# Dilated attention scores in one piece per unit, and a new projection order, in a two-layer hybrid encoder

## The chip, the cores and the metric

The kernel runs on one core of a Trainium2 chip. The metric is the device time of one launch in microseconds (us). Three runs of the kernel before the change took 927.87, 928.56 and 929.92 us; the median, 928.56 us, is the number that the change is measured against.

## The reference

Two encoder layers over 512 positions of width 1024, then a final RMSNorm. A layer normalizes x, projects it once into many parts, runs two attention branches over them, gates each branch and projects back:

```python
h = rms_norm(x, norm_g[layer])
p = h @ w_in[layer]
c_q, c_kv, k_r, gate_a, dil_qkv, gate_b = jnp.split(p, split_points, axis=-1)
a = mla_attention(c_q, c_kv, k_r, ...) * jax.nn.silu(gate_a)
b = dilated_attention(dil_qkv, cos_d, sin_d) * jax.nn.silu(gate_b)
x = x + jnp.concatenate([a, b], axis=-1) @ w_out[layer]
```

The latent branch has 8 heads; queries and keys come from low-rank latents (384 and 256 wide) that get an RMSNorm of their own. The dilated branch has 3 groups of 8 heads of 64, with windows and dilations (128, 1), (512, 4) and (2048, 16); the groups' outputs are weighted by their softmax denominators and added. Everything is float32, to float32 accuracy.

## The kernel before, in words

Activations lie transposed: chunks of 128 features by 512 positions. To keep accuracy, each operand is split into a high and a low part (ACT makes the high part at L221, DVE the low part at L222), and each product is three matmuls (`triple`, L241 to L243: high by high, high by low, low by high). So a projection of 128 output features from 1024 inputs is 24 matmuls of 512 columns in one PSUM bank. PSUM has 8 banks, and all of them come from one pool (`bank()`, bufs=8): who asks for a ninth waits until the oldest has been read.

Weights are fetched three tiles ahead of their use (`prefetch`, L188 to L205, AHEAD = 3): SP loads the raw tile (L195), ACT makes the high part (L198), and the low part comes either from DVE (L203) or, for the projections in `ADDED` after the place `FROM` in the plan, from ACT (L200) and an accumulating transfer on the POOL queue (L201).

Dilated heads go in units: 12 in a layer, each with two heads of one group. Units of the first group are "near" (`near_scores` L653, `near_out`), of the other two "far" (`far_scores` L727, `far_out` L769). For each unit the main line makes the queries and the keys (`dil_qk`); there is one buffer of keys (`kst`), so the next unit's keys wait until this unit's scores are done. The scores are matmuls with 64 rows (L673 near; L744 and L747 far), two heads beside each other in two banks. A unit's scores come in two parts: a near part is 12 matmuls, a far part 8, each with 2 banks. DVE and ACT then turn scores into exponentials (L680, L750, L753 and others). The outs transpose the exponentials (L449), split them again (`pt`, L221 and L222) and multiply them with the values (L550 near, L785 far); a far unit has four such products, and behind each of them ACT copies half of a bank (L788) and DVE adds twice (L789, L791). `combine` (L818) and `combine_last` (L837) weight and add the groups. `mla_out` does the same for a pair of latent heads ("mo").

At the end of a layer `out_part` (L849) projects the mixed outputs, 24 matmuls to a chunk of x, and `out_add` (L840) takes the result: it fetches the old chunk into one of two buffers (`xl`, bufs=2), adds (DVE, L845), stores (L846), makes the high part (ACT, L273) and the low part (DVE, L274) for the next layer, and squares it (ACT, L264; added up on POOL, L268). The next layer begins with `latent_first` (L364): its matmuls (L376) take the eight chunks one after the other as they come.

The order of all this on TensorE is not that of the layers' formulas. `Weave.run` (L84 to L136) takes the projections from a main line, in the order that `forward_order()` (L29, L30) lists, and puts the other work between them from side lines: norms (`nline`), scores (`sline`), outs (`tline`), and combinations with the latent outputs among them (`cline`). A task on a side line is released when what it needs was finished a given lag ago, counted in modelled microseconds (LD 8.25 for dilated scores, LM 2.0 for latent scores, LG 6.0 and LG2 16.5 for outs, LAG 2.5 for most others), and a credit (RATE, CAP) limits how much side work may stand between projections. Where the main line is blocked, side tasks go ahead of their lags (`force`). Inside a side line the order is fixed, so a task that is not ready holds up those behind it.

At the start eleven matmuls on zeros (L296, WARM) run while the first loads arrive. ACT's queue issues the load of the first raw weights, of the norm gains (`gn`), and of the second raw weights.

Of the kernel before, what the change touches and what calls it, by code (L numbers as in the profile page):

```python
# [7 lines left out]
F32 = mybir.dt.float32  # L8
# [3 lines left out]
ALU = mybir.AluOpType  # L12
# [11 lines left out]
STEP, LD0, WARM, LG2, LY = 2, 10.0, 11, 16.5, 5.0  # L24
LV = 3.0
# [3 lines left out]
def forward_order():  # L29
    return [('ckv',), ('v', 1, 0), ('cq', 2), ('cq', 0), ('cq', 1), ('dqk', 0, 0), ('dqk', 0, 1), ('nv', 0), ('mur', 0), ('ga', 0), ('dqk', 1, 0), ('kr',), ('dqk', 1, 1), ('nv', 1), ('muq', 0), ('muk', 0), ('mv', 0), ('muq', 1), ('dqk', 2, 1), ('muk', 1), ('dqk', 2, 0), ('muq', 2), ('dqk', 3, 1), ('muq', 3), ('dqk', 3, 0), ('dqk', 4, 1), ('mur', 1), ('v', 2, 0), ('muq', 4), ('dqk', 4, 0), ('dqk', 5, 0), ('muk', 2), ('ga', 1), ('muq', 5), ('dqk', 5, 1), ('mv', 1), ('dqk', 6, 0), ('nv', 2), ('gb', 0), ('muq', 6), ('dqk', 6, 1), ('muq', 7), ('nv', 3), ('dqk', 8, 0), ('gb', 1), ('muk', 3), ('v', 1, 1), ('ga', 2), ('dqk', 7, 0), ('dqk', 7, 1), ('dqk', 10, 0), ('dqk', 8, 1), ('dqk', 9, 0), ('dqk', 9, 1), ('v', 2, 1), ('dqk', 10, 1), ('ga', 3), ('dqk', 11, 0), ('dqk', 11, 1), ('gb', 2), ('gb', 3)]  # L30
# [27 lines left out]
FROM = PLAN.index(("dqk", 0, 1, 1))  # L58
# [79 lines left out]
def hybrid_encoder(ctx, tc, xT, wst, gains, fgain, tables, keytab, masks, out):  # L138
# [9 lines left out]
    def t(shape, dtype, tag, bufs):  # L148
        uid[0] += 1
        return sb.tile(shape, dtype, name=f"{tag}_{uid[0]}", tag=tag, bufs=bufs)  # L150
# [137 lines left out]
    load_w(nc.scalar, 0)  # L288
    nc.scalar.dma_start(gn, gains)
    load_w(nc.scalar, 1)  # L290
# [362 lines left out]
    def near_scores(L, u, part):  # L653
# [5 lines left out]
        if part == 0:  # L659
            L.st0[p] = t([128, 4, 4], F32, "st0", 2)  # L660
        st = L.st0[p]
        banks = [bank() for _ in range(2)]
        for j in range(2):
            i = 2 * part + j
# [9 lines left out]
        for j in range(2):  # L674
            i = 2 * part + j
# [11 lines left out]
        if part:  # L687
            by_residue(L, p)
        yield 0.9, 1.0
# [37 lines left out]
    def far_scores(L, u, part):  # L727
# [7 lines left out]
        pt = t([128, S], F32, "p", 8)  # L735
        p4 = pt.rearrange("p (j a x) -> p j a x", j=2, a=2)
        banks = [bank() for _ in range(2)]
        by4 = lambda x: x.rearrange("p j (x y) -> p j x y", y=4)
        for j in range(2):
            b = 2 * part + j  # L740
# [7 lines left out]
        for a in range(2):  # L748
# [394 lines left out]
```

## Time and profile before

| what | value |
|---|---|
| median of three runs | 928.56 us (927.87 to 929.92) |
| the profiled execution, its own time | 929.99 us |
| span of its instructions | 928.2 us |
| mean granted TensorE clock | 0.996 |

The page's first part gives each engine's busy time as a share of the span. A row of a list of instructions has the start in us, the time from start to end in us, the engine, the line, the operation, what it writes and reads, and how many equal ones follow each other (x12); a bracket at its end is a wait just before it and what ended it. A row of the waits has the sum of a releaser's waits in us, their number, and the mean. A row of the grouped instructions has the sum of busy us and the mean ns of one, then the idle us before them. In the list by tiles three numbers stand for the shortest, the median and the longest ns.

### The profile page before, as it was taken

To read this page: it belongs to the slowest core of one execution; us is meant where nothing else is said; L and a number is where in the kernel's file an instruction comes from. 1 tells how busy PE (TensorE), PEld (TensorE's weight loads), DVE (VectorE), ACT (ScalarE), POOL (GpSimd) and SP (SyncE) were. 2 spreads that over 40 slices of the span, in tenths; PEclk is the share of its full clock that TensorE was granted. 3 is DMA by queue.
4 is the path that set the end of the run, shared out by engine and by line. 5 is a ranking of instruction groups with operands and counts; after the bars stand their busy time and mean duration, and the time that the engine had idled before them with its cause. 6 is when DMAs were issued, how large, how long until landed. Compare 5 with 4: busy or idle time off the path is not lost.

```text
span 928.2 us, 15855 instructions
## 1 busy us (share of the span) xinstructions
PE 908.0 (98%) x5175; PEld 773.4 (83%) x5175; DVE 692.4 (75%) x1733; ACT 597.6 (64%) x1449; POOL 313.2 (34%) x365
## 2 busy tenths in 40 slices
PE   9999999999999999999999999999999999999996
PEld 7978888988889889887897888889888888898785
DVE  6756787877868776688766679787878676767964
ACT  6546876667757766764445468756768586676533
POOL 0134253345542432233211343524464234224300
PEclk9999999999999999999999999999999999999998
DMA  8457453276554764664453653615667558367542
GB/s 271 121 124 146 97 123 69 65 163 148 122 124 93 148 125 107 137 155 132 166 169 95 146 121 82 126 40 134 138 126 158 129 101 167 78 142 138 147 125 91
DMA packets 86466, 118.14 MB, mean 127 GB/s; under 512 B 16944, under 2 KB 37232, under 8 KB 86384
## 3 DMA queue, kind: packets, MB, share of 16 engines
q1 hardware_dynamic: 66656, 81.59, 30.6%
q0 software_dynamic: 19296, 35.14, 24.0%
q8 instruction: 41, 0.67, 0.3%
q10 hardware_dynamic: 432, 0.41, 0.1%
q14 instruction: 41, 0.34, 0.1%
HBM read 112.74 MB, written 4.36 MB: 126 GB/s over the span
## 4 chain that ended last, share of the span: by engine, by line
PE 83%; DVE 8%; ACT 4%; issue 2%; DMA 1%; POOL 1%; ACTq 0%; DVEq 0%; POOLq 0%
PE bank L241 22%; PE bank L242 22%; PE bank L243 22%; PE bank L449 5%; PE bank L550 3%; PE bank L376 3%; PE bank L744 1%; PE bank L785 1%; PE bank L673 1%; DVE pt L222 1%; DVE whl L203 1%; ACT whl L198 1%; DMA p<-wst 1%; DMA wraw<-wst 1%; DVE tmp L630 1%
## 5 line engine op out<-in xcount | busy, mean ns | idle before, releaser
L241 PE MATMUL bank<-hl,whl 128*128 128x512 f32 x712 | 283.9, 399 | 2.2 <-ACT hl L221 1.3
L242 PE MATMUL bank<-hl,whl 128*128 128x512 f32 x712 | 278.3, 391 | 0.0
L243 PE MATMUL bank<-hl,whl 128*128 128x512 f32 x712 | 278.1, 391 | 0.0
L198 ACT CAST whl<-wraw 128x512 fp32r<-128x512 f32 (+3 forms) x243 | 143.8, 596 | 121.2 <-PE bank L243 80.2
L201 POOL DMA_DIRECT2D whl<-wst x134 | 117.9, 884 | 225.2 <-ACT whl L200 152.7
L243 PEld LDWEIGHTS bank<-hl,whl 128*128 128x128 f32 x712 | 133.6, 188 | 29.5 <-DMA whl<-wst 0.4
L241 PEld LDWEIGHTS bank<-hl,whl 128*128 128x128 f32 x712 | 133.7, 188 | 28.5 <-ACT hl L221 1.7
L242 PEld LDWEIGHTS bank<-hl,whl 128*128 128x128 f32 x712 | 134.0, 188 | 23.9 <-DVE hl L222 0.3
L241 PE MATMUL bank<-whl,hl 128*128 128x256 f32 (+2 forms) x328 | 99.6, 304 | 1.6 <-ACT hl L221 1.6
L243 PE MATMUL bank<-whl,hl 128*128 128x256 f32 (+2 forms) x328 | 97.9, 298 | 0.0
L242 PE MATMUL bank<-whl,hl 128*128 128x256 f32 (+2 forms) x328 | 97.7, 298 | 0.0
L628 POOL TENSOR_TENSOR tmp<-tmp,sd 128x512 f32<-128x512 f32 x48 | 63.2, 1316 | 91.9 <-DVE tmp L626 65.4
L203 DVE TENSOR_TENSOR whl<-wraw,whl 128x512 fp32r<-128x512 f32 (+3 forms) x109 | 76.6, 710 | 23.1 <-ACT whl L198 22.1
L222 DVE TENSOR_TENSOR pt<-bank,pt 128x512 fp32r<-128x512 f32 x128 | 83.6, 684 | 5.4 <-ACT pt L221 4.0
L200 ACT ACTIVATE whl<-wraw 128x512 fp32r<-128x512 f32 x134 | 85.0, 634 | 0.1
L221 ACT CAST pt<-bank 128x512 fp32r<-128x512 f32 x128 | 69.9, 588 | 10.7 <-PE bank L449 10.3
L530 POOL TENSOR_SCALAR p<-p,lc 128x512 f32<-128x512 f32 x64 | 48.8, 769 | 70.0 <-DVE lc L529 64.2
L449 PE MATMUL bank<-ident,p 128*128 128x128 f32 x512 | 67.7, 275 | 0.0
L241 PEld LDWEIGHTS bank<-whl,hl 128*128 128x128 f32 x328 | 62.3, 190 | 3.9 <-ACT hl L221 1.8
L243 PEld LDWEIGHTS bank<-whl,hl 128*128 128x128 f32 x328 | 62.3, 190 | 2.0 <-DVE hl L222 0.4
L242 PEld LDWEIGHTS bank<-whl,hl 128*128 128x128 f32 x328 | 62.4, 190 | 1.7
L449 PEld LDWEIGHTS bank<-ident,p 128*128 128x128 f32 x512 | 59.2, 142 | 5.4
(181 smaller groups left out, 1620.1 us busy)
## 6 DMA issues: line engine op xcount, KB each, us to landing
wraw<-wst SPq DMA_DIRECT2D x218, 256.0 KB, 3.1
whl<-wst POOLq DMA_DIRECT2D x134, 256.0 KB, 4.4
tmp<-shd SPq DMA_DIRECT2D x32, 128.0 KB, 4.3
xl<-xT SPq DMA_DIRECT2D x10, 256.0 KB, 2.9
wraw<-wst SPq DMA_DIRECT2D x16, 144.0 KB, 2.3
wraw<-wst SPq DMA_DIRECT2D x12, 192.0 KB, 2.6
x1d<-xl SPq DMA_DIRECT2D x8, 256.0 KB, 3.2
xl<-x1d SPq DMA_DIRECT2D x8, 256.0 KB, 3.2
```

Source lines behind the costliest of these rows:

```text
L198: nc.scalar.copy(hi, src)
L200: nc.scalar.mul(lo, src, -1.0)
L201: nc.gpsimd.dma_start(lo, wst[emitted[0], :, :c], accum_op=ALU.add)
L203: nc.vector.tensor_tensor(lo, src, F(hi), op=ALU.subtract)
L221: nc.scalar.copy(dst_hi, src)
L222: nc.vector.tensor_tensor(dst_lo, src, F(dst_hi), op=ALU.subtract)
L241: nc.tensor.matmul(a, w[:, 0], h[:, 0], start=first, stop=False)
L242: nc.tensor.matmul(a, w[:, 0], h[:, 1], start=False, stop=False)
L243: nc.tensor.matmul(a, w[:, 1], h[:, 0], start=False, stop=last)
L449: nc.tensor.transpose(b[:, 128 * i:128 * i + 128], x, ident)
L530: nc.gpsimd.tensor_scalar(pt, pt, l1, 0.0, op0=ALU.mult, op1=ALU.add)
L628: nc.gpsimd.tensor_tensor(u, u, L.sd, op=ALU.mult)
```

## The change

It has four parts.

1. **Scores of a dilated unit as one piece.** `near_scores` and `far_scores` no longer take a part: all 24 or 16 matmuls are issued in a row into four banks, and after them the vector work of both halves. The modelled cost that they report is that of two parts (1.8 and 0.9).
2. **Scores don't wait for values.** The scores of a latent head no longer need its values ("mv"), those of a dilated unit no longer need "v" or "nv". The outs need the values instead, with a lag LO = 4.0. The norm of the query latents waits a lag LQ = 5.0 after its projections, not LAG = 2.5. The latent outputs ("mo") get a line of their own (`gline`).
3. **Another list in `forward_order()`**, of the same projections. `FROM` is now the later of the first two key projections, and in the second layer the place of `load_ahead` is the later of ("gb", 2) and ("muq", 7).
4. **Start.** The load of `gn` goes out on the POOL queue, so ACT's queue has only the two loads of weights; WARM is 10, not 11.

In the parts of the diff below, the new list of projections is shown only by its start.

```diff
-STEP, LD0, WARM, LG2, LY = 2, 10.0, 11, 16.5, 5.0
-LV = 3.0
+STEP, LD0, WARM, LG2, LY = 2, 10.0, 10, 16.5, 5.0
+LV, LQ, LO = 3.0, 5.0, 4.0
...
-    return [('ckv',), ('v', 1, 0), ('cq', 2), ('cq', 0), ('cq', 1), ('dqk', 0, 0), ('dqk', 0, 1), ('nv', 0), ...
+    return [('ckv',), ('v', 1, 0), ('cq', 2), ('dqk', 0, 1), ('cq', 0), ('cq', 1), ('dqk', 0, 0), ('dqk', 1, 0), ...
...
-FROM = PLAN.index(("dqk", 0, 1, 1))
+FROM = max(PLAN.index(("dqk", 0, i, 1)) for i in range(2))
...
-    load_w(nc.scalar, 0)
-    nc.scalar.dma_start(gn, gains)
-    load_w(nc.scalar, 1)
+    nc.gpsimd.dma_start(gn, gains)
+    for k in range(2):
+        load_w(nc.scalar, k)
...
-    def far_scores(L, u, part):
+    def far_scores(L, u):
...
-        pt = t([128, S], F32, "p", 8)
-        p4 = pt.rearrange("p (j a x) -> p j a x", j=2, a=2)
-        banks = [bank() for _ in range(2)]
+        pts = [t([128, S], F32, "p", 8) for _ in range(2)]
+        both = [[bank() for _ in range(2)] for _ in range(2)]
...
-        for j in range(2):
-            b = 2 * part + j
+        for b in range(4):
+            banks, j = both[b // 2], b % 2
...
-        yield 0.44, 0.5
+        yield 0.9, 1.0
...
-    main, nline, sline, tline, cline = ([] for _ in range(5))
+    main, nline, sline, tline, cline, gline = ([] for _ in range(6))
...
-        task(nline, k("lcq"), later(*[k("cq", c) for c in range(3)], k("norm")), latent_norm, "cq")
+        task(nline, k("lcq"), [(k("cq", c), LQ) for c in range(3)] + later(k("norm")), latent_norm, "cq")
...
-                task(sline, k("s0", what, n), [(x, LM if what == "m" else LD0 if n == 0 else LD) for x in needs], scores, n, 0)
-                task(sline, k("s", what, n), now(*before[0]), scores, n, 1)
-                task(tline, k("o", what, n), [(k("s", what, n), LG2 if what == "d" and unit(n)[0] == 2 else LG)], f, n)
+                needs = [(x, LM if what == "m" else LD0 if n == 0 else LD) for x in needs]
+                if what == "m":
+                    task(sline, k("s0", what, n), needs, scores, n, 0)
+                    task(sline, k("s", what, n), now(*before[0]), scores, n, 1)
+                else:
+                    task(sline, k("s", what, n), needs + now(*before[0]), scores, n)
+                g, p = unit(n) if what == "d" else (0, 0)
+                values = k("mv", n // 4) if what == "m" else k("v", g, p // 2) if g else k("nv", p)
+                task(tline, k("o", what, n), [(k("s", what, n), LG2 if g == 2 else LG), (values, LO)], f, n)
...
-                task(cline, k(what, n), needs, f, n)
+                task(gline if what == "mo" else cline, k(what, n), needs, f, n)
```

What this does to the order can be read off the two programs. The number of matmuls on TensorE is the same but for the one on zeros: 5174 for 5175. The pieces of scores become fewer: 46 runs of score matmuls before, 24 after, one for each of the 12 units of two layers. Of the 46, four near units were in one piece of 24 already and four in two pieces of 12; 14 far units were in two pieces of 8 and two in three.

The first place is the scores of the last far unit of layer 0 on TensorE. Before, the second part of the scores (`bank_4888`, `bank_4889`) stands behind an out of another unit (L785) and the rest of a projection (L241 to L243 into `bank_4823`):

```order
L744 MATMUL bank_4849<-kst,q_4678 128x256
L744 MATMUL bank_4850<-kst,q_4678 128x256
L747 MATMUL bank_4849<-kst,q_4678 128x128
L747 MATMUL bank_4850<-kst,q_4678 128x128
L785 MATMUL bank_4869<-pt_4727,v_3594 128x256 x2
L241 MATMUL bank_4823<-hl_172,whl_4759 128x512
L242 MATMUL bank_4823<-hl_172,whl_4759 128x512
L243 MATMUL bank_4823<-hl_172,whl_4759 128x512
L241 MATMUL bank_4823<-hl_178,whl_4759 128x512
L242 MATMUL bank_4823<-hl_178,whl_4759 128x512
L243 MATMUL bank_4823<-hl_178,whl_4759 128x512
L744 MATMUL bank_4888<-kst,q_4678 128x256
```

After, the second half (`bank_4863`, `bank_4864`) follows the first (`bank_4861`, `bank_4862`) at once:

```order
L740 MATMUL bank_4861<-kst,q_4643 128x256
L740 MATMUL bank_4862<-kst,q_4643 128x256
L743 MATMUL bank_4861<-kst,q_4643 128x128
L743 MATMUL bank_4862<-kst,q_4643 128x128
L740 MATMUL bank_4863<-kst,q_4643 128x256
L740 MATMUL bank_4864<-kst,q_4643 128x256
L743 MATMUL bank_4863<-kst,q_4643 128x128
L743 MATMUL bank_4864<-kst,q_4643 128x128
```

What moved is the projection work that stood between the two halves; it now stands around the whole piece.

The second place is TensorE at the end of layer 0, where the last two far units' outs are (L785 before, L783 after; `pt` are split exponentials, `v` the values). Before, the four products of the last unit have output projections (L241 to L243) between them:

```order
L785 MATMUL bank_5173<-pt_5122,v_4389 128x256 x2
L785 MATMUL bank_5180<-pt_5122,v_4389 128x256 x2
L785 MATMUL bank_5187<-pt_5130,v_4389 128x256 x2
L241 MATMUL bank_4962<-hl_5147,hl_5009 128x512
L242 MATMUL bank_4962<-hl_5147,hl_5009 128x512
L243 MATMUL bank_4962<-hl_5147,hl_5009 128x512
L241 MATMUL bank_4980<-hl_5147,hl_5045 128x512
L242 MATMUL bank_4980<-hl_5147,hl_5045 128x512
L243 MATMUL bank_4980<-hl_5147,hl_5045 128x512
L785 MATMUL bank_5194<-pt_5130,v_4389 128x256 x2
```

After, the outs of units 10 and 11 follow each other, with only the transposes of unit 11 (L449) between them:

```order
L783 MATMUL bank_5107<-pt_5040,v_3647 128x256 x2
L783 MATMUL bank_5114<-pt_5040,v_3647 128x256 x2
L783 MATMUL bank_5121<-pt_5048,v_3647 128x256 x2
L783 MATMUL bank_5128<-pt_5048,v_3647 128x256 x2
L449 MATMUL bank_5135<-ident,p_4859 128x128 x4
L449 MATMUL bank_5143<-ident,p_4860 128x128 x4
L783 MATMUL bank_5152<-pt_5140,v_3648 128x256 x2
L783 MATMUL bank_5159<-pt_5140,v_3648 128x256 x2
L783 MATMUL bank_5166<-pt_5148,v_3648 128x256 x2
L783 MATMUL bank_5173<-pt_5148,v_3648 128x256 x2
L241 MATMUL bank_5180<-hl_2194,whl_5075 128x512
L242 MATMUL bank_5180<-hl_2194,whl_5075 128x512
```

Projections that stood between these outs stand earlier in the layer now. Five sums of output projections (`bank_4841`, `bank_4928`, `bank_4964`, `bank_4989` and `bank_5017`) are open all through these rows, so three of the eight banks go round: a row's bank is free once that of the third row above it has been read, and `bank_5180` once DVE's second add has read `bank_5159`. Right behind, where layer 1 begins: before, 115 matmuls of 512 columns stand between the last output projection of x's first chunk and the first use of its last chunk by layer 1. After, 77 of 512 and 26 of 288 columns stand there.

More of the change, by code (lines that the diff above doesn't have):

```diff
@@ L651, in dil_qk, with near_scores @@
         yield 0.65 * STEP, 0.0
-    def near_scores(L, u, part):
+    def near_scores(L, u):
         g, p = unit(u)
         q = L.q["d", u]
-        if part == 0:
-            L.st0[p] = t([128, 4, 4], F32, "st0", 2)
-        st = L.st0[p]
-        banks = [bank() for _ in range(2)]
-        for j in range(2):
-            i = 2 * part + j
+        st = L.st0[p] = t([128, 4, 4], F32, "st0", 2)
+        both = [[bank() for _ in range(2)] for _ in range(2)]
+        for i in range(4):
+            banks, j = both[i // 2], i % 2
             for x, (lq, lk) in enumerate(((0, 0), (0, 1), (1, 0))):
@@ L673, in near_scores @@
                     nc.tensor.matmul(so, q[r, lq, 128 * i:128 * i + 128], k, start=x == 0, stop=x == 2)
-        for j in range(2):
-            i = 2 * part + j
+        for i in range(4):
+            banks, j = both[i // 2], i % 2
             m = msk[:, 0:256] if i else msk[:, 256:512]
@@ L686, in near_scores @@
             L.p["d", u, i] = pt
-        if part:
-            by_residue(L, p)
-        yield 0.9, 1.0
+        by_residue(L, p)
+        yield 1.8, 1.0
     def by_residue(L, p):
@@ L734, in far_scores @@
         m = msk[:, 512:640].rearrange("p (x y) -> p x y", y=4) if g == 1 else msk[:, 640:644].unsqueeze(1).to_broadcast([128, 32, 4])
-        pt = t([128, S], F32, "p", 8)
-        p4 = pt.rearrange("p (j a x) -> p j a x", j=2, a=2)
-        banks = [bank() for _ in range(2)]
+        pts = [t([128, S], F32, "p", 8) for _ in range(2)]
+        both = [[bank() for _ in range(2)] for _ in range(2)]
         by4 = lambda x: x.rearrange("p j (x y) -> p j x y", y=4)
-        for j in range(2):
-            b = 2 * part + j
+        for b in range(4):
+            banks, j = both[b // 2], b % 2
             c = slice(128 * b, 128 * b + 128)
@@ L747, in far_scores @@
                 nc.tensor.matmul(so, q[64 * a:64 * a + 64, 1, c], kst[64 * a:64 * a + 64, 0, c], start=False, stop=True)
[L748 to L760 removed]
+        for part in range(2):
+            p4 = pts[part].rearrange("p (j a x) -> p j a x", j=2, a=2)
+            for a in range(2):
+                s = both[part][a].rearrange("p (j l x) -> p j l x", j=2, l=2)
+                nc.vector.tensor_tensor(by4(p4[:, :, a]), by4(s[:, :, 0]), m.unsqueeze(1).to_broadcast([128, 2, 32, 4]), op=ALU.add)
+                for j in range(2):
+                    b = 2 * part + j
+                    nc.vector.tensor_tensor_reduce(p4[:, j, a], s[:, j, 1], p4[:, j, a], -0.125, 3e38, ALU.add, ALU.min,
+                                                   st[:, b, a:a + 1])
+                for j in range(2):
+                    b = 2 * part + j
+                    nc.scalar.activation(p4[:, j, a], p4[:, j, a], AF.Exp, scale=-1.0, bias=st[:, b, a:a + 1],
+                                         accum_out=st[:, b, 2 + a:3 + a])
+            L.p["d", u, part] = pts[part]
+        if g == 2:
             shares(L, p)
@@ L998, in hybrid_encoder @@
         if last:
[L999 removed]
+            at = [i for i, x in enumerate(main) if x[0] in (k("gb", 2), k("muq", 7))][-1]
             line = []
```

21 lines of the change are left out of this document (4 added, 17 removed).

## The prediction

> **What bounds the kernel now.** I read the page first: which engine is busy.
>
> ```profile
> span 928.2 us, 15855 instructions
> PE 908.0 (98%) x5175; PEld 773.4 (83%) x5175; DVE 692.4 (75%) x1733; ACT 597.6 (64%) x1449; POOL 313.2 (34%) x365
> ```
>
> TensorE (PE) is busy for 908.0 of 928.2 us, and no other engine for more than 75%. So a gain can only come from PE's own time, which is not all at full rate, and from the 20 us around it. What PE waits for is in the second view, its waits by releaser; the ten longest are:
>
> ```profile
> PE bank L241 <- ACT hl L221: 2.9, 2, 1.6
> PE bank L256 <- POOL tmp L354: 1.8, 2, 0.9
> PE bank L296 <- DVE q L293: 1.5, 1, 1.5
> PE bank L744 <- ACT q L221: 1.4, 2, 0.7
> PE bank L550 <- ACT pt L221: 1.2, 2, 0.6
> PE bank L747 <- DVE q L222: 1.1, 2, 0.5
> PE bank L550 <- DVE pt L222: 0.9, 2, 0.4
> PE bank L241 <- DVE st L680: 0.9, 1, 0.9
> PE bank L785 <- DVE og L791: 0.7, 2, 0.4
> PE bank L376 <- ACT hl L273: 0.6, 2, 0.3
> ```
>
> All are small and come twice, once for each layer: the order leaves too little work between a producer and PE's use. A new order can take away each one, or put another in its place. The third view is PE's instructions one by one around scores:
>
> ```profile
> 237.65 0.39 PE L242 MATMUL bank<-hl,whl 128*128 128x512 f32 x1
> 237.88 0.39 PE L243 MATMUL bank<-hl,whl 128*128 128x512 f32 x1
> 238.19 0.38 PE L744 MATMUL bank<-kst,q 64*128 64x256 f32 x2
> 238.42 0.22 PE L747 MATMUL bank<-kst,q 64*128 64x128 f32 x2
> ...
> 238.64 0.22 PE L747 MATMUL bank<-kst,q 64*128 64x128 f32 x2
> 238.79 0.50 PE L241 MATMUL bank<-hl,whl 128*128 128x512 f32 x1
> 239.13 0.40 PE L242 MATMUL bank<-hl,whl 128*128 128x512 f32 x1
> ```
>
> Matmuls of 512 columns follow each other every 0.23 us, though each lasts 0.39 (the end overlaps the next). So a wait costs its idle time and about 0.16 us more, since the overlap is lost. A far piece of 8 takes 239.13 - 237.88 = 1.25 us, in which two matmuls of 512 (0.46) are; 0.79 is left. Of this a block (four matmuls) takes 0.22 (238.42 to 238.64); the rest is what entering and leaving the 64-row form costs.
>
> **The change, part by part.** The sum is made against the profiled execution's 929.99 us, which is 1.43 above the median.
>
> *Scores in one piece.* A far piece of 16 is 0.79 + 2 x 0.22 = 1.23 instead of 2 x 0.79 = 1.58: 0.35 saved, for 16 far units 5.6 us; the two third pieces save about 0.3 each, 0.6. The near pieces:
>
> ```profile
> 291.80 0.98 PE L673 MATMUL bank<-kst,q 64*128 64x256 f32 x12
> 292.71 0.50 PE L785 MATMUL bank<-pt,v 128*128 128x256 f32 x2
> ...
> 81.01 1.69 PE L673 MATMUL bank<-kst,q 64*128 64x256 f32 x24
> 82.63 0.50 PE L241 MATMUL bank<-hl,whl 128*128 128x512 f32 x1
> ```
>
> Twelve take 0.91, so two pieces 1.82; twenty-four take 1.62, and each piece has some 0.2 around it that is then paid once: 0.4 for each of 4 units, 1.5. Together -7.7. If the edges were half as dear it would be -5, with dearer near edges -8.5.
>
> *Waits in mid-layer.* Scores that don't need values, the lag LQ and the new order part the producers from their uses: the waits at L256, L744, L747, L550 (both) and L241 behind L680 are 1.8 + 1.4 + 1.1 + 1.2 + 0.9 + 0.9 = 7.3 us in 11 places. In the new order each of these pairs has 3 us or more of PE work between, where the longest of these waits is 0.9. With 11 x 0.16 that is -9.1. If a third stays under another name, -6.
>
> *Half clock.* The windows view has one dip of the granted clock, behind two such waits in layer 0; its twin in layer 1 has none:
>
> ```profile
> 135.00:140.00 5.00, 5.00 (x25) 0.67 0.55 97
> 131.53 0.38 PE L744 MATMUL bank<-kst,q 64*128 64x256 f32 x2
> 132.45 0.33 PE L747 MATMUL bank<-kst,q 64*128 64x128 f32 x2 [0.54 <-DVE q L222]
> 133.77 1.23 PE L550 MATMUL bank<-pt,v 128*128 128x256 f32 x7 [0.45 <-DVE pt L222]
> 138.75 0.40 PE L241 MATMUL bank<-kml,q 96*128 96x512 f32 x1
> ...
> 586.76 0.38 PE L744 MATMUL bank<-kst,q 64*128 64x256 f32 x2
> 592.43 0.39 PE L241 MATMUL bank<-kml,q 96*128 96x512 f32 x1
> ```
>
> In the first row the fourth number is the granted clock, 0.67. The same work takes 7.22 us here and 5.67 in layer 1. With the waits gone, so is the dip: -1.5, or 0 if the clock drops somewhere else.
>
> *Start.* `gn` is second on ACT's queue, and the first high part waits for it:
>
> ```profile
> 5.55 0.72 ACT L273 ACTIVATE hl<-og,gn 128x512 fp32r<-128x512 f32 x1 [1.11 <-DMA gn<-gains]
> 6.32 2.35 PE L376 MATMUL bank<-hl,hl 128*128 128x512 f32 x9 [0.32 <-ACT hl L273]
> ```
>
> PE's first projection follows that ACT instruction at once. On POOL's queue `gn` has nothing ahead of it, and the second raw weights move up one place. But what comes next, the weights and chunks, arrives hardly earlier, and PE had only 0.32 idle here. I take -0.3, between 0 and -0.6. The warm-up matmul left out ran in time that waits anyway: 0. POOL and ACT have nothing else queued then.
>
> *Ends of the layers.* The waits at L241 behind L221 (2.9, 2) and at L785 (0.7, 2) lie there, since outs of the last units stand too close; with 4 x 0.16 that is -4.2, as these spots are ordered anew. In their place:
>
> ```profile
> L789 DVE TENSOR_TENSOR tmp<-bank,tmp 64x256 f32<-64x256 f32 x64 | 26.9, 420 | 10.6 <-ACT tmp L788 9.6
> L791 DVE TENSOR_TENSOR og<-bank,tmp 64x256 f32<-64x256 f32 x64 | 26.9, 420 | 1.7
> L222 DVE TENSOR_TENSOR pt<-bank,pt 128x512 fp32r<-128x512 f32 x128 | 83.6, 684 | 5.4 <-ACT pt L221 4.0
> L837 DVE TENSOR_TENSOR og<-og,og 128x512 f32<-128x512 f32 x8 | 5.5, 686 | 0.2
> ...
> 438.42 0.87 PE L785 MATMUL bank<-pt,v 128*128 128x256 f32 x6
> 439.49 0.87 DVE L789 TENSOR_TENSOR tmp<-bank,tmp 64x256 f32<-64x256 f32 x2
> ...
> L845 DVE TENSOR_TENSOR xl<-xl,bank x8: 680/689/691, 447.2 to 469.2; 128x512 f32<-128x512 f32 x8
> L273 ACT ACTIVATE hl<-xl,gn x8: 709/724/727, 448.0 to 469.9; 128x512 fp32r<-128x512 f32 x8
> ```
>
> At layer 0's end the outs of units 10 and 11 now stand back to back, with three banks to go round. The projection behind them gets its bank when DVE has made 12 adds (12 x 0.42), two low parts (2 x 0.684) and one combination (0.686): 7.1 us. From the first product to DVE's first add are 439.49 - 438.42 = 1.07, and some 0.5 goes in gaps for ACT's copies: 8.6. PE's own work there, 16 products and 8 transposes, is 24 x 0.12 = 2.9 (six products take 0.87, the last one's end included). Stall: +5.7. It would be 3 if ACT and DVE overlap better than I take it, 8 if DVE is late with earlier work.
>
> At layer 1's start, x's eight chunks go through two buffers: from the first add at 447.2 to the end of the last high part, 469.9 + 0.72 = 470.6, are 23.4 us. Before, PE had 115 matmuls of 512 in that time (26.5 us) and waited only for the 0.6 at L376 shown above. After, it has 77 of 512 and 26 of 288 columns, 17.7 + 3.4 = 21.1. Stall: 23.4 + 0.4 for the ends of the first and last step - 21.1 = +2.7; 0 if the loads through the two buffers run faster with less beside them, 5 if the adds come later by the stall ahead.
>
> Not shown by the trace of before: new small waits at layer 1's end (0 to 1.6, I take 0.8), three spots in mid-layer where a producer is under 2 us ahead (0 to 3, 1.0), and a clock dip. For that the nearest row is the dip above: it came behind gaps of only 0.54 and 0.45, and cost 1.5; once, and not at its twin. The stretch of 9 us at layer 0's end has several gaps of about 1 us, so I take half of it: +0.8, between 0 and 1.7. The Trainium skill ("TensorE: Matmul & The Clock Gate", Part 1, "The HAM clock gate") has the half rate come only after an idle window of about 3.4 us. By that rule the new gaps would cost no clock, and the sum would be 0.8 lower; the row speaks against it, as no gap near it is over 0.54 us.
>
> Sum: -7.7 - 9.1 - 1.5 - 0.3 - 4.2 + 5.7 + 2.7 + 0.8 + 1.0 + 0.8 = -11.8. So 918.2 for the profiled execution, 916.8 against the median.
>
> **The rivals.**
>
> *Banks (slower).* A joined piece takes four of eight banks at once and gives back none before DVE has gone through the first. The price is in the waits: L241 behind L680 of a near unit's scores, 0.9 idle and 0.16. If each of the 20 newly joined units (16 far, 4 near) did this, it would be 20 x 1.06 = +21 us: 938. It turns the sign from 11 such waits on (11 x 1.06 = 11.7). For it: in the output projections five banks are held anyway. Against: in the new order the first bank asked back after a piece has at least 14 matmuls (3.2 us) ahead of it, and before, the one with 2.4 us of work waited 0.9 and those at 3.1 didn't. The Trainium skill ("TensorEngine Tiling (Array Packing)", "Gotcha 1: PSUM Pressure") warns that tiling by rows takes more banks at once; the one wait of 0.9 agrees. Chance 0.10.
>
> *Bunching gives half back.* Where outs and scores are in larger lumps, DVE, ACT and PE take turns at the ends of both layers, not of one. If layer 1's end, which has the same outs and output rows, stalls as layer 0's does (+5.7 instead of 0.8) and the chunks take their 5 instead of 2.7, that is +7.2: 924. For it: DVE is at 75%, and a unit's 8 adds come in one lump. Against: in layer 1 no next layer waits, and the order there has projections between the last outs. Chance 0.16.
>
> *The ends are cheap.* If the stall at layer 0's end is 3, layer 1's start costs nothing, and no small wait or dip comes up, it is -2.7 - 2.7 - 2.6 = 8 us less: 909. Chance 0.12.
>
> *The change does not do what it says.* The order of the changed program has the 24 pieces whole, so I give this nothing.
>
> **How the numbers follow.** My forecast has 0.62; its own range is 912 to 922, from the joined pieces (1.7 either way), the waits (2), the end of layer 0 (2.5), the start of layer 1 (2.5) and the rest (1.5), which are independent: the root of the sum of squares is 4.7. For 8 times in 10 the range also takes in the cheap ends and the bunching, with their own spread of about 2.5: 907 to 927. Left out are the banks (0.10) and some 0.08 at the edges. About 0.2% is what a measurement of this kernel tells from no change, so faster is below 926.7: the forecast 0.62, the cheap ends 0.12 and three quarters of the bunching, 0.86. The same (926.7 to 930.4): the rest of the bunching and a little of the banks, 0.05. Slower: the banks, 0.09.
>
> **What would show it.** In the changed profile: a piece of 16 far scores takes about 1.2 us, one of 24 near 1.6; PE's busy time falls by about 9 us (pieces and clock); the waits at L256, at the scores and at L550 are gone. At the end of layer 0 PE stands for 5 to 6 us among the outs of units 10 and 11, released by L222 and by DVE's reads of banks, and at the start of layer 1 L376 waits 2 to 3 us for L273. No other line has a wait of a joined piece's bank. I am wrong if the pieces save less than 5 us, if waits for banks stand behind most of the joined units, or if the stalls at the ends pass 15 us together.

## The result: 2.9% slower, and the profile after

The changed kernel took 955.55 us (median of 4 runs, 953.94 to 959.56) against 928.74 us before on the same chip; the ratio is 1.0294 with a 95% interval from 1.0275 to 1.0313. The forecast was 916.8 us. The profiled execution, whose lines follow, took 959.56 us and is the slowest of the four, at a mean granted clock of 0.982; the others had 0.985 to 0.987. By estimate its loss by the clock is 3 to 5 us more than theirs.

The page of the changed kernel:

```profile
span 957.7 us, 15886 instructions
PE 915.2 (96%) x5174; PEld 777.1 (81%) x5174; DVE 699.9 (73%) x1733; ACT 594.9 (62%) x1449; POOL 313.9 (33%) x366
```

Before, 928.2 - 908.0 = 20.2 us of the span were without PE work; now it is 957.7 - 915.2 = 42.5, 22.3 more. And PE is busy for 7.2 us more, though it has the same matmuls but for one of the warm-up. So there are two losses: PE waits more, and it works more slowly. PE's waits (sum in us, number, and the longest in us; the reading help ahead of the prediction calls the last number the mean, but it is the longest):

```profile
PE bank L243 <- DMA whl<-wst: 13.3, 5, 5.1
PE bank L376 <- ACT hl L273: 2.8, 2, 1.5
PE bank L241 <- POOL q L512: 2.5, 3, 1.4
PE bank L241 <- ACT hl L221: 2.1, 2, 1.9
PE bank L449 <- ACT ku L819: 1.5, 1, 1.5
PE bank L783 <- DVE st L751: 1.5, 1, 1.5
PE bank L296 <- DVE q L293: 1.5, 1, 1.5
PE bank L783 <- DVE og L789: 1.5, 1, 1.5
PE bank L243 <- DVE q L222: 1.4, 2, 0.8
PE bank L817 <- DVE st L751: 1.1, 1, 1.1
```

Of the waits that the forecast meant to lose in mid-layer, L256, both at L550 and L241 behind the near units' scores are gone; at the far units' scores (L740, before L744 and L747) 1.7 of 2.5 us are left, in other places. In their place stands a group of which the kernel before had 0.4 us: the third matmul of a triple, L243, waits for the low part of a weight tile (13.3 us in 5 places), which the accumulating transfer on the POOL queue brings. All of PE's waits together are 34.4 us in 29 places, before 13.0 in 18.

The slower work is in the windows of 5 us (length of the window, busy time of PE, PEld, DVE, ACT and POOL with counts, then granted clock, DMA share, GB/s):

```profile
85.00:90.00 5.00, 3.60 (x12) 2.90 (x12) 1.71 (x3) 0.90 (x3) 3.22 (x4) 0.64 0.83 175
90.00:95.00 5.00, 5.00 (x20) 4.22 (x20) 3.05 (x10) 2.58 (x7) 1.89 (x3) 0.68 0.20 35
...
445.00:450.00 5.00, 4.23 (x15) 3.08 (x14) 4.80 (x10) 2.18 (x6) 0.00 (x0) 0.50 0.00 0
...
725.00:730.00 5.00, 3.40 (x9) 2.82 (x10) 3.08 (x5) 2.03 (x4) 2.25 (x3) 0.50 0.94 205
```

Leaving out the end of each program, where PE has almost no work, twelve of the windows lie at 0.98 or less, in five groups, each behind waits of PE; before there was one (0.67). Busy time times the clock that is missing, summed over them, is an estimate of what that costs: 12.6 us, before 1.7. So the account of the profiled 29.5 us is: idle +22.3, clock +10.9, eleven more restarts at 0.16 +1.8, shorter score pieces -7.1; that makes 27.9, and 1.6 us are not assigned.

The pieces themselves are close to the forecast. PE at a far unit and at a near one:

```profile
212.75 0.40 PE L243 MATMUL bank<-hl,whl 128*128 128x512 f32 x1
213.07 0.39 PE L740 MATMUL bank<-kst,q 64*128 64x256 f32 x2
...
214.14 0.50 PE L241 MATMUL bank<-hl,whl 128*128 128x512 f32 x1
214.48 0.40 PE L242 MATMUL bank<-hl,whl 128*128 128x512 f32 x1
...
262.82 1.69 PE L671 MATMUL bank<-kst,q 64*128 64x256 f32 x24
264.44 0.39 PE L241 MATMUL bank<-whl,hl 128*128 128x256 f32 x1
```

214.48 - 212.75 = 1.73, less two matmuls of 512 (0.46), is 1.27 us for sixteen (forecast 1.23, two pieces of eight 1.58). Twenty-four near ones take 1.62.

How a weight comes too late shows best at 253 us. PE, then ACT, then POOL there:

```profile
248.90 0.40 PE L242 MATMUL bank<-hl,whl 128*128 128x512 f32 x1
252.99 0.50 PE L243 MATMUL bank<-hl,whl 128*128 128x512 f32 x1 [3.69 <-DMA whl<-wst]
```

```profile
242.82 0.63 ACT L200 ACTIVATE whl<-wraw 128x512 fp32r<-128x512 f32 x1
```

```profile
243.89 1.29 POOL L628 TENSOR_TENSOR tmp<-tmp,sd 128x512 f32<-128x512 f32 x1 [4.74 <-DVE e L808]
245.16 3.66 POOL L763 TENSOR_SCALAR p<-p,e 128x128 f32<-128x128 f32 x8
248.78 0.84 POOL L201 DMA_DIRECT2D whl<-wst  x1
```

ACT has the negated weight ready at 242.82 + 0.63 = 243.45. But in POOL's rows a rotation (L628), which waited 4.74 us for DVE, and the eight scalings of a last group's exponentials (L763) stand ahead of the transfer. The transfer is issued at 248.78, 5.3 us late, and lands at 253: PE waits 3.7. In layer 1 the same spot costs 5.1. The other three waits for weights (0.9, 1.8 and 1.7 us) are not of this kind: there the transfer goes out 0.3 us after ACT's negated copy (L200 ends at 78.06, the transfer starts at 78.36), so the weight is late from the load or from ACT.

### The profile page after: what moved, and what is told of

Read it like the earlier page. It is cut to its first block, busy times and chain, and to the rows that moved or that the text cites. A ratio compares the mean times of both kernels' runs of the same rounds, so it can differ in the third digit from the quotient of the medians.

```text
span 957.7 us, 15886 instructions
## 1 busy us (share of the span) xinstructions
PE 915.2 (96%) x5174; PEld 777.1 (81%) x5174; DVE 699.9 (73%) x1733; ACT 594.9 (62%) x1449; POOL 313.9 (33%) x366
## 4 chain that ended last, share of the span: by engine, by line
PE 74%; DVE 8%; DMA 6%; issue 5%; ACT 4%; POOL 2%; SPq 0%; POOLq 0%; DVEq 0%; ACTq 0%
PE bank L241 20%; PE bank L243 20%; PE bank L242 19%; PE bank L449 5%; PE bank L550 3%; PE bank L376 2%; DMA whl<-wst 2%; DVE whl L203 1%; DMA tmp<-shd 1%; PE bank L671 1%; PE bank L783 1%; DVE pt L222 1%; ACT p L755 1%; PE bank L740 1%; DMA shd<-ku 1%
## 5 line engine op out<-in xcount | busy, mean ns | idle before, releaser
L243 PE MATMUL bank<-hl,whl 128*128 128x512 f32 x712 | 281.0, 395 | 13.3 <-DMA whl<-wst 13.3
L241 PE MATMUL bank<-hl,whl 128*128 128x512 f32 x712 | 287.0, 403 | 0.2 <-DVE st L751 0.2
L201 POOL DMA_DIRECT2D whl<-wst x134 | 118.9, 887 | 254.1 <-ACT whl L200 202.2
L243 PEld LDWEIGHTS bank<-hl,whl 128*128 128x128 f32 x712 | 134.8, 189 | 45.3 <-DMA whl<-wst 16.1
L241 PEld LDWEIGHTS bank<-hl,whl 128*128 128x128 f32 x712 | 135.0, 190 | 25.5 <-PE bank L817 0.3
L222 DVE TENSOR_TENSOR pt<-bank,pt 128x512 fp32r<-128x512 f32 x128 | 84.3, 685 | 26.7 <-ACT pt L221 25.5
L241 PE MATMUL bank<-whl,hl 128*128 128x256 f32 (+2 forms) x328 | 99.8, 304 | 1.9 <-ACT hl L221 1.9
L243 PE MATMUL bank<-whl,hl 128*128 128x256 f32 (+2 forms) x328 | 97.8, 299 | 0.0
L203 DVE TENSOR_TENSOR whl<-wraw,whl 128x512 fp32r<-128x512 f32 (+3 forms) x109 | 82.5, 761 | 18.9 <-ACT whl L198 18.3
L628 POOL TENSOR_TENSOR tmp<-tmp,sd 128x512 f32<-128x512 f32 x48 | 64.4, 1341 | 94.4 <-DVE tmp L626 83.7
L200 ACT ACTIVATE whl<-wraw 128x512 fp32r<-128x512 f32 x134 | 84.7, 632 | 0.1
L221 ACT CAST pt<-bank 128x512 fp32r<-128x512 f32 x128 | 69.8, 586 | 10.0 <-PE bank L449 7.9
L449 PE MATMUL bank<-ident,p 128*128 128x128 f32 x512 | 69.3, 278 | 2.5 <-ACT ku L819 1.5
L449 PEld LDWEIGHTS bank<-ident,p 128*128 128x128 f32 x512 | 61.0, 144 | 10.5 <-issue 3.4
L755 ACT ACTIVATE p<-p,st 128x128 f32<-128x128 f32 x128 | 49.8, 390 | 29.9 <-DVE st L751 29.8
L241 PEld LDWEIGHTS bank<-whl,hl 128*128 128x128 f32 x328 | 62.3, 190 | 4.2 <-ACT hl L221 2.3
L242 PEld LDWEIGHTS bank<-whl,hl 128*128 128x128 f32 x328 | 62.4, 190 | 2.4 <-DVE whl L203 0.9
```

The lines of the kernel that those rows point to most:

```text
L200: nc.scalar.mul(lo, src, -1.0)
L201: nc.gpsimd.dma_start(lo, wst[emitted[0], :, :c], accum_op=ALU.add)
L203: nc.vector.tensor_tensor(lo, src, F(hi), op=ALU.subtract)
L221: nc.scalar.copy(dst_hi, src)
L222: nc.vector.tensor_tensor(dst_lo, src, F(dst_hi), op=ALU.subtract)
L241: nc.tensor.matmul(a, w[:, 0], h[:, 0], start=first, stop=False)
```

## The experiments

Theories, as the expectations name them: LIST (the new list makes the loss), LUMPS (the joined scores do), NEEDS (the new needs do), QUEUE or LEAD (weights come late on POOL's queue, or with too short a lead), COMBINE (DVE waits for a combination's transfers), COVER (the layers' ends lack work), and TUNED (each part is harmless, but any order that isn't fitted to the measured durations loses).

**The new start alone.** The kernel before with

```diff
+    nc.gpsimd.dma_start(gn, gains)
     load_w(nc.scalar, 0)
-    nc.scalar.dma_start(gn, gains)
     load_w(nc.scalar, 1)
```

and WARM 10.

> The kernel before with the new start alone (the gains' load on the POOL queue, ten matmuls on zeros instead of eleven). By the forecast 0.3 us less, between 0 and 0.6: the ratio lies within 0.2% of 1. If the load of the gains comes later on POOL's queue than on ACT's, the first high part waits longer than its 1.11 us, and it is 0.5 to 2 us more.

Measured: 929.99 us against 929.78, ratio 1.0001 (0.9991 to 1.0012). This part is nothing.

**The old list in the changed kernel, and split scores in the changed kernel.** The first has the list of before:

```diff
-    return [('ckv',), ('v', 1, 0), ('cq', 2), ('dqk', 0, 1), ('cq', 0), ('cq', 1), ...
+    return [('ckv',), ('v', 1, 0), ('cq', 2), ('cq', 0), ('cq', 1), ('dqk', 0, 0), ...
```

The second has `near_scores` and `far_scores` with parts, and two tasks for each unit again:

```diff
-                if what == "m":
-                    task(sline, k("s0", what, n), needs, scores, n, 0)
-                    task(sline, k("s", what, n), now(*before[0]), scores, n, 1)
-                else:
-                    task(sline, k("s", what, n), needs + now(*before[0]), scores, n)
+                task(sline, k("s0", what, n), needs, scores, n, 0)
+                task(sline, k("s", what, n), now(*before[0]), scores, n, 1)
```

> The changed kernel with the list of projections of before; joined scores, the new needs and lags, and the new start stay. If the new list makes the time (theory LIST: its neighbours put the low parts of weights on the POOL queue behind other work, and leave no cover at the ends), the waits at L243 for the weights' transfer go (13.3 us with the clock behind them), and with the joined pieces' 7 us kept the time is 918 to 930. If the joined scores make it (theory LUMPS: lumps of vector work on DVE and ACT delay what is queued behind them, in whatever list), the waits for weights stay and it is over 940.

> The changed kernel with the scores of a dilated unit in two parts again, all else as changed. By LIST the pieces cost 7 us more and the waits stay: 955 to 965. By LUMPS the waits for the weights' transfers (13.3 us) and the clock behind them (about 8) go, less 7 for the pieces: 935 to 945.

Measured: the old list 948.49 (ratio 1.0196, 1.0177 to 1.0216), split scores 984.91 (1.0585, 1.0547 to 1.0623). The first came out as LUMPS had it (8.0 us of waits for weights stay), the second as neither theory had it. With the old list most of the loss stays, so the list alone does not make it; with split scores it grows by 29 us, so in this order the joined pieces alone don't make it either. PE's longest waits of the run with split scores:

```profile
PE bank L785 <- DVE v L222: 17.9, 2, 9.1
PE bank L241 <- DVE st L753: 9.7, 3, 4.6
PE bank L241 <- POOL q L512: 5.0, 4, 1.5
```

Waits for weights are 0.3 us in all here: outs stand ahead of their values and banks are late. Every version has waits of its own.

**Joined scores alone, and new needs alone,** in the kernel before. The first is the reverse of the diff above, with the changed `near_scores` and `far_scores`; the second is part 2 of the change.

> The kernel before with the joined scores alone (list, needs, lags and start of before). The two kernels with the old list so far differ by 19 us (929.7 before, 948.5 with joined scores, new needs and new start). If the lumps of vector work make that (theory LUMPS), this is 940 to 950. If they don't, the pieces' 7 us are left: 920 to 926.

> The kernel before with the new needs and lags alone (scores don't wait for values, LQ, LO, latent outputs on their own line); list, split scores and start of before. If scores that go out earlier make the 19 us (theory NEEDS: they come right behind the queries' projection, and banks and buffers are held longer), this is 940 to 950. By LUMPS it is 926 to 932.

Measured: joined scores alone 945.52 (1.0186, 1.0157 to 1.0214), new needs alone 942.45 (1.0146, 1.0114 to 1.0177). Each alone costs 13 to 17 us, both together (the run with the old list) 19. That speaks for LUMPS and NEEDS at once, or for something that both have in common: both change the order. (There is no run of the new list with the old needs: the keys of the third unit would wait for scores that wait for values standing later in the list.)

**A control: the kernel before with a little of its order changed.** Two neighbours of the list exchanged, and one lag:

```diff
-    ... ('muk', 0), ('mv', 0), ...
+    ... ('mv', 0), ('muk', 0), ...
```

```diff
-LG, LP, LD, LM, LC, LN, LX, LF = 6.0, 0.25, 8.25, 2.0, 14.25, 5.75, 5.0, 0.25
+LG, LP, LD, LM, LC, LN, LX, LF = 6.5, 0.25, 8.25, 2.0, 14.25, 5.75, 5.0, 0.25
```

> The kernel before with two neighbours of its list exchanged (the first latent values ahead of the first latent keys). Nothing of the change is in it. Theory TUNED: the list of before is fitted to its durations so closely that any edit of the order puts a few weight transfers, banks or outs late; then this small edit alone costs 3 to 15 us, 932 to 945. If the parts of the change are bad by themselves (LUMPS, NEEDS), an exchange of neighbours costs under 2 us: 928 to 931.

> The kernel before with the lag LG at 6.5, not 6.0: outs go out half a microsecond of modelled time later, in an order that differs in most of the program. TUNED: slower by 5 to 20 us, 934 to 949, with waits at L243 for the weights' transfer that the kernel before does not have. LUMPS, NEEDS: 927 to 932, since nothing is joined and no need is changed.

Measured: the exchange 928.76 (0.9995, 0.9982 to 1.0009), nothing, where TUNED had 3 to 15 us; the lag 955.40 (1.0276, 1.0256 to 1.0296). Half a modelled microsecond on the lag of the outs costs as much as the whole change. The exchange moves work in two short stretches, the lag in most of the program. PE's longest waits with the lag at 6.5:

```profile
PE bank L785 <- DVE pt L222: 5.0, 1, 5.0
PE bank L785 <- DVE el L806: 4.1, 1, 4.1
PE bank L550 <- DVE pt L222: 4.0, 4, 1.4
PE bank L744 <- ACT q L221: 2.7, 4, 0.7
```

TUNED had waits for weights here; they are only 1.3 us. The loss is even above the 5 to 20 us that it gave, and the place is another.

**Taking the waits for weights away, in two ways.** In the first, four tiles of each layer, those that PE waited for and the next one, get their low part from DVE; in the second, weights are fetched one tile earlier, into one more buffer:

```diff
+LATE = {("dqk", 1, 1, 1), ("dqk", 8, 0, 0), ("nv", 3, 0), ("nv", 3, 1)}
-            if key[0] in ADDED and i > FROM:
+            if key[0] in ADDED and i > FROM and key not in LATE:
```

```diff
-AHEAD, RATE, LAG, CAP = 3, 451.1, 2.5, 34.9
+AHEAD, RATE, LAG, CAP = 4, 451.1, 2.5, 34.9
-        return t([128, 2, 512], FR, "whl", 4)
+        return t([128, 2, 512], FR, "whl", 5)
```

> The changed kernel, but in each layer four weight tiles (those that TensorE waits for, and the one behind the last of them) get their low part from DVE (L203), not from the accumulating transfer on the POOL queue; values are the same. If the POOL queue is what makes them late (theory QUEUE), the 13.3 us at L243 and most of the clock loss behind them go: 930 to 937. If DVE and ACT are late themselves (theory LATE ENGINES), the waits come back at L242 or L243 behind L203, and it is over 945.

> The changed kernel with the weights fetched four tiles ahead, not three, and five buffers for them, not four. If the lead of the weights is what is short (theory LEAD: a low part by POOL takes a load, two copies on ACT, what stands ahead on POOL's queue, and 4.7 us of transfer), the waits at L243 for the transfer (13.3 us) and the clock behind them go: 930 to 938. If the vector work is late in itself, the waits come back as waits for banks or for L222, as in the run with the low parts on DVE: 950 to 956.

Measured: low parts by DVE 955.43 (1.0273, 1.0256 to 1.0290), the longer lead 950.89 (1.0228, 1.0205 to 1.0250). Of the 13.3 us of waits nothing is left in the first and 0.2 in the second. Yet the first leaves the time where it was, and the second takes off some 6 of the 27 us; all of PE's waits together are still 28.8 and 31.7 us. PE at the same place with the low parts by DVE (all lines are one further there: L672 is the near scores' matmul, L790 the second addition of a far out):

```profile
256.19 1.91 PE L672 MATMUL bank<-kst,q 64*128 64x256 f32 x12 [1.34 <-ACT whl L201]
258.73 0.55 PE L672 MATMUL bank<-kst,q 64*128 64x256 f32 x1 [0.63 <-ACT pt L222]
260.96 1.61 PE L672 MATMUL bank<-kst,q 64*128 64x256 f32 x11 [1.69 <-DVE og L790]
```

PE now starts the near unit's scores at 256.19, not 262.82, and ends them at 262.5, not 264.4: of 6.6 us 1.9 are left. The second and third wait are for banks that ACT (L222) and DVE (L790) have yet to read; the first is put down to L201, which reads no bank, and the trace says no more of it. In layer 1 the same piece waits 1.05 and 1.39 us for L790. This is the rival of the banks, at two places, behind a wait that had covered it. With the longer lead it is the same:

```profile
PE bank L671 <- DVE og L789: 3.1, 3, 2.2
PE bank L671 <- ACT whl L200: 1.7, 1, 1.7
...
PE bank L243 <- DMA whl<-wst: 0.2, 1, 0.2
```

So QUEUE describes what PE waits for, but not all that limits this stretch: behind POOL's queue DVE and ACT are late as well.

**The longer lead in the kernel before,** by the same edit.

> The kernel before with the weights fetched four tiles ahead and five buffers. It has only 0.4 us of waits for weights, so the longer lead has nothing to win: 926 to 930 if it does no harm. By TUNED it moves work on ACT, DVE and POOL forward against the rest and costs 3 us or more.

Measured: 935.73 (1.0064, 1.0041 to 1.0086). A longer lead with 0.4 us of waits to win costs 6 us.

**Three edits of the changed kernel for single suspects:** a gate behind the last keys, the latent outputs back on the line of the combinations, and the lag LY.

```diff
-    ... ('v', 1, 1), ('gb', 2), ('dqk', 9, 1), ... ('dqk', 11, 1), ('gb', 3)]
+    ... ('v', 1, 1), ('dqk', 9, 1), ... ('dqk', 11, 1), ('gb', 2), ('gb', 3)]
```

```diff
-                task(gline if what == "mo" else cline, k(what, n), needs, f, n)
+                task(cline, k(what, n), needs, f, n)
```

```diff
-STEP, LD0, WARM, LG2, LY = 2, 10.0, 10, 16.5, 5.0
+STEP, LD0, WARM, LG2, LY = 2, 10.0, 10, 16.5, 11.0
```

> The changed kernel with one projection, the gate ("gb", 2), behind the last dilated unit's keys as in the list of before. If the ends of the layers lack cover (theory COVER), their 48 matmuls of 512 columns stand under the last outs, and of the 7 us lost at layer 0's end and the 8 at layer 1's end a half goes: 945 to 950. If the ends are bound by the vector work itself, the 48 matmuls are merely elsewhere: 953 to 958.

> The changed kernel with the latent outputs back on the line of the combinations. Theory COMBINE: on a line without the latent outputs ahead of them, the combinations go out earlier, and DVE, which takes its instructions in order, stands at L829 until the shares are back from memory (15.4 us in 6 waits, 9.6 in 7 before), with what is queued behind it. Then this takes 5 to 10 us off the 955. If the waits have nothing to do with the line, it is 953 to 958.

> The changed kernel with the lag LY between the issue of a combination's transfers and the multiplication that needs them at 11.0, not 5.0. Theory COMBINE: DVE's waits at L829 (15.4 us) go, and with them what they make late: the waits for weights at 253 and 727 us with the clock behind them (about 13 us): 940 to 946. If DVE's wait there only fills time, the scores and weights behind it are late all the same: 952 to 958.

Measured: 958.89 (1.0310, 1.0274 to 1.0346), 954.65 (1.0276, 1.0253 to 1.0299) and 955.89 (1.0292, 1.0275 to 1.0309). None helps. With the gate at the end, the waits for weights are 15.5 us; that its cover is missing where it stood before is not shown. The last two were no test of what COMBINE says of the time, since DVE's waits at L829 stayed: 14.4 us with the latent outputs moved back and 15.8 with the lag, 15.4 in the changed kernel. That the separate line makes these waits is not borne out; whether they cost time is left open.

**The order fitted anew.** If the parts are harmless, an order that fits them must win. In the kernel before with joined scores (its needs, its start), the constants were set anew and some ten projections moved by a few places, by the durations of the traces:

```diff
-AHEAD, RATE, LAG, CAP = 3, 451.1, 2.5, 34.9
-STEP, LD0, WARM, LG2, LY = 2, 10.0, 11, 16.5, 5.0
-LV = 3.0
-LG, LP, LD, LM, LC, LN, LX, LF = 6.0, 0.25, 8.25, 2.0, 14.25, 5.75, 5.0, 0.25
+AHEAD, RATE, LAG, CAP = 4, 338.6, 3.25, 33.9
+STEP, LD0, WARM, LG2, LY = 2, 10.0, 11, 15.0, 4.25
+LV = 3.5
+LG, LP, LD, LM, LC, LN, LX, LF = 5.75, 0.11, 7.0, 4.0, 11.25, 8.0, 3.25, 0.0
```

The weights have five buffers here. Split scores and the changed kernel were fitted in the same way, with values of their own.

> The kernel before with joined scores (needs, start and the line of latent outputs as before), weights four tiles ahead, 14 lags and constants of the weave set anew, and some ten projections of the list a few places earlier or later, so that each release stands at least as far behind what it waits for as the traces say it must. Theory TUNED (the parts are harmless, the order has to fit them): the waits of the run with joined scores alone (30.4 us) fall to about 12, under those of the kernel before, and the pieces' 7 us are kept: 914 to 924, faster than before. If joined scores are bad in themselves: 935 to 945.

> The kernel before, scores in two parts as before, fitted anew in the same way (four tiles ahead, 12 lags and constants, some ten places of the list). TUNED: waits fall to about 10 us, but the pieces' 7 us aren't there: 918 to 928, and 4 to 8 us more than the fitted kernel with joined scores. If joined scores are bad in themselves, this is the faster of the two by 10 us or more.

> The changed kernel, with all its parts, with 16 lags and constants set anew and some ten projections of its list moved a few places. TUNED: the waits for weights (13.3 us) and most of the clock loss go, a part of the ends' stalls stays, since the list still leaves one projection behind the last keys: 926 to 942. If the list or the needs are bad in themselves: 948 or more.

Measured: joined scores 923.55 (0.9935, 0.9921 to 0.9950), split scores 941.73 (1.0128, 1.0112 to 1.0144), the changed kernel 945.32 (1.0167, 1.0149 to 1.0186). The first is the one version here that is faster than the kernel before. Its page and its longest waits (its L566 is L550 of before):

```profile
PE 901.3 (98%) x5175; PEld 771.7 (84%) x5175; DVE 705.5 (77%) x1733; ACT 592.5 (64%) x1449; POOL 314.2 (34%) x365
```

```profile
PE bank L566 <- ACT pt L237: 2.3, 2, 1.2
PE bank L566 <- DVE pt L238: 2.3, 6, 0.6
PE bank L731 <- ACT pt L237: 1.8, 1, 1.8
```

PE is busy 6.7 us less than before (908.0). Some 1.7 of that is the dip of the clock at 135 us, which this execution does not have; the 5 that are left fit the pieces, if a little short of 7. Its waits are 11.8 us, with none for a weight. The other two missed: the fit for split scores was to be 918 to 928, that of the changed kernel 926 to 942. So a fit by durations is not reliable, and the joined scores can't be judged by these two kernels beside each other. The next pair does that.

**The same fitted order with scores split, and with one lag half a microsecond longer** (LG 6.25 for 5.75).

> The kernel with the order fitted to joined scores, list and lags kept, but with the scores in two parts again. If a joined piece is worth what the rows say (0.35 us a unit) and the order minds little: 928 to 933, 7 us more. By TUNED the parts shift everything behind them against the fitted lags, and it is 935 or more.

> The kernel with the order fitted to joined scores, with the lag LG at 6.25, not 5.75. By TUNED this loses like the kernel before did by the same step (26 us there): 933 to 950, with waits in places that the fitted order has none. If the fitted order has more room, 922 to 928.

Measured: split 930.05 (1.0014, 1.0000 to 1.0027), the lag 936.19 (1.0079, 1.0062 to 1.0095). Beside 0.9935 the joined pieces are worth 0.79%, 7.3 us, in which 2.3 us of waits are (14.1 in the profiled execution with split scores, 11.8 with joined). That is what the rows said for an order that minds little; TUNED had 935 or more. The fitted order loses 1.4%, 13 us, by the same small step of LG as the kernel before. So both orders are sensitive to this lag, as TUNED has it, but not to every edit: the exchange cost nothing, and split scores no more than the pieces.

## Why the prediction was wrong, point by point

- **Score pieces, -7.7: right.** By the changed profile 0.31 for each of 16 far units; with 0.6 for the third pieces and 1.5 for the near ones, as forecast, -7.1. By the pair of fitted orders -7.3, some waits included.
- **Waits in mid-layer, -9.1: those named did go.** But the step behind it, "In the new order each of these pairs has 3 us or more of PE work between", covers only the pairs that had waited before. **This step failed.** The pairs that had not waited were taken as safe but for three spots, and the longest new waits are at pairs taken as safe: for the tiles of ("dqk", 1, 1) and ("nv", 3) in both layers and of ("dqk", 8, 0) in layer 1, 13.3 us in 5 places. Nor are these waits the bound by themselves: without them (low parts by DVE) others come up, and the time is the same. Besides, the distance was counted in PE's work, while at the one place followed above the work ahead in another engine's queue decided: at 253 us the weight's chain began in time and stood 5.3 us behind POOL's own instructions.
- **New small waits, +1.0 in mid-layer:** the term that was too small. It was sized by spots with a producer under 2 us ahead. Measured are 13.3 for weights, 2.5 for L512 and 1.4 for L222 behind the latent queries, 1.1 at L817 and some small ones: about 19 us in place of 1.
- **Clock, -1.5 and +0.8:** the old dip went, and five new ones came, of 1.3 to 3.0 us each: +10.9. The half of a dip that was put at one place was a whole one at five. And the old dip was not a sure gain: with the new start alone, an execution of the old order has the same two waits and no dip (the rows are in the last section).
- **Start, -0.3:** nothing. On POOL's queue the gains' load is no earlier: the first high part starts at 6.14 us, with the new start alone at 5.74, before at 5.55.
- **End of layer 0, +5.7, and start of layer 1, +2.7: right in size.** From the first product of unit 10 to the projection behind unit 11:

```profile
440.38 0.87 PE L783 MATMUL bank<-pt,v 128*128 128x256 f32 x6
442.73 0.47 PE L783 MATMUL bank<-pt,v 128*128 128x256 f32 x2 [1.48 <-DVE og L789]
...
444.66 1.03 PE L449 MATMUL bank<-ident,p 128*128 128x128 f32 x4 [0.85 <-DVE og L789]
445.75 2.13 PE L783 MATMUL bank<-pt,v 128*128 128x256 f32 x6
448.48 0.77 PE L783 MATMUL bank<-pt,v 128*128 128x256 f32 x2 [0.59 <-ACT tmp L786]
449.04 0.66 PE L241 MATMUL bank<-hl,whl 128*128 128x512 f32 x1
```

449.04 - 440.38 = 8.66 us, forecast 8.6: three banks to go round, and DVE's adds in order. The same stretch in two halves, as windows:

```profile
440.38:444.66 4.28, 1.96 (x13) 1.40 (x12) 3.52 (x9) 2.05 (x5) 0.00 (x0) 1.00 0.57 188
444.66:449.04 4.38, 3.61 (x12) 2.65 (x13) 4.16 (x9) 1.69 (x4) 0.00 (x0) 0.51 0.00 0
```

DVE, which sets the pace, is busy for 7.7 of the 8.66 us. PE is idle for 3.1, not for 5 to 6, as its own work in the second half ran at a granted clock of 0.51 and filled the rest. At layer 1's start PE waits 1.32 us at 481 for L273, 0.59 at 485 for a weight and 0.90 at 491 for L274, 2.8 together. (The 0.6 us at L376 that the prediction puts there for the kernel before are at 6.3 and 8.9 us, at the start of layer 0; layer 1's start had no wait. Nor do all ten of those waits come twice: the ones at L296 and behind L680 come once.)
- **Ends of the layers, -4.2, and end of layer 1, +0.8: too good.** In layer 1 PE waits 1.5 at L783, 1.5 at L449 and 1.9 at L241, with smaller ones 6 us: the size that the rival of the bunching had put there (5.7). The 1.9 is the wait behind L221 of the kernel before (1.6 at 875 us), which the forecast had counted as gone.
- **The rival of the banks** had the right sign and 938 us, with a chance of 0.10. That it met the sign is luck: in the changed kernel waits that can be for banks of joined pieces are 3.6 us at most (0.8 at L740, 2.8 behind L751, which reads the scores), not 21. More of them exist, as the two runs without waits for weights show, but behind others.

What is shown: joined pieces are worth some 7 us in an order fitted to them, the start is nothing, and the loss is PE's waits and the clock behind them, which the new order brings and which no single part of the change makes alone. Four edits of the kernel before that move work through most of the program (joined scores, new needs, one lag, the whole change) cost 13 to 27 us each, a fifth (the longer lead) 6, whatever they were meant to do; an exchange of neighbours cost nothing. What is not settled: whether the new list with the new needs has a fit that beats the kernel before, since the one that was tried took 945.32; a fit of the old order with split scores lost as well (941.73); and why the lags allow so little, beyond that the waits come up at other places each time.

## What to carry to other kernels

In a kernel whose order is fitted by hand to measured durations, look at the pairs that do not wait yet: the slack of every producer, counted in the queue of the engine that makes it, is what a reorder spends. Before trusting a gain from a reorder, time more than one control that moves the order by a trifle: here one cost nothing and another 2.8%. If such an edit alone costs 3%, a part is better judged by taking it out of an order that was fitted to it, as with the split scores here. And a wait that is taken away is only worth the distance to the next one behind it.

## What the runs showed of the hardware

The granted clock fell behind short gaps of PE, and not behind all of them. In the changed kernel PE had gaps of 0.91 and 1.40 us at 84 to 86 us, and the clock was at 0.64 and 0.68 in the next ten. After gaps of 1.50 and 1.53 us at 898 and 903 us no window up to 950 us lies under 0.99. The Trainium skill ("TensorE: Matmul & The Clock Gate", Part 1, "The HAM clock gate") has the clock halved after an idle window of about 3.4 us; the dips behind 0.91 and 1.40 don't agree with that, and the measurement decides.

Nor does one place have its dip each time. The kernel before had 0.67 at 135 to 140 us, behind waits of 0.54 and 0.45. With the new start alone, the same two waits are there 0.8 us earlier, and the clock of the window (the number ahead of the last two) is 1.00:

```profile
131.65 0.33 PE L747 MATMUL bank<-kst,q 64*128 64x128 f32 x2 [0.54 <-DVE q L222]
132.97 1.22 PE L550 MATMUL bank<-pt,v 128*128 128x256 f32 x7 [0.45 <-DVE pt L222]
135.00:140.00 5.00, 5.00 (x28) 4.18 (x28) 4.62 (x21) 4.41 (x19) 0.00 (x0) 1.00 0.42 83
```

What decides between the two is not shown.

A DVE instruction that takes 0.68 us (median of L203) took 2.49, in both layers at the same place, beside a POOL instruction that had started within it:

```profile
78.60 2.49 DVE L203 TENSOR_TENSOR whl<-wraw,whl 128x512 fp32r<-128x512 f32 x1 [0.28 <-ACT whl L198]
```

```profile
78.36 0.86 POOL L201 DMA_DIRECT2D whl<-wst  x1 [5.75 <-DVE tmp L497]
78.94 1.60 POOL L498 TENSOR_TENSOR tmp<-tmp,cms 128x512 f32<-128x512 f32 x1
```

Behind it on DVE stand the latent query's rotation and its split, and PE's waits for that query at 86 us. The Trainium skill ("SBUF — State Buffer", "SBUF: two separate sides") says that DVE and GpSimd hold a shared port pair for a whole instruction, and the other blocks. Here 2.49 is about 0.68 and 1.60 together, 2.28, which agrees with a block. But by that section whichever starts first keeps the ports, and in these rows DVE's record starts 0.34 us ahead of POOL's, so the order does not agree; no run took the pair apart.
